# A streaming encoder layer on one core: stores issued by ScalarE, value matmuls of two heads paired, one compare split in two, projections copied out of PSUM first

## The chip, the core and the metric

One Trainium2 chip, one of its NeuronCores. The metric is the device time of one execution in microseconds (us), lower is better; shown are the median and the extremes of several executions, and one further execution that the hardware profiler recorded. Engines: PE (TensorE), DVE (VectorE), ACT (ScalarE), POOL (GpSimd), SP (SyncE, here only an issuer of DMAs).

## What is computed

One layer of an encoder for a prompt of 1024 rows (8 tiles of 128) and a decode batch of 8 x 16 rows (tile 8), model width 1024:

```python
n1 = rmsnorm(h); q_a,k_a,v_a,fl,q_b,k_b,v_b,gate_a,gate_b = split(n1 @ w_in)
y_a = forgetting attention, 8 heads x 64: softmax(q k / 8 + sum of log f) v, causal; decode reads a cache of 2048
y_b = chunk-band attention, 8 heads x 64: own chunk of 64 and the 8 before; decode reads a cache of 512
h += (sigmoid(gate_a) * (y_a @ w_up_a) + sigmoid(gate_b) * (y_b @ w_up_b)) @ w_out
h += PEER(rmsnorm(h))        # 128^2 single-neuron experts, 8 heads, the best 16 each
h += sigmoid(rmsnorm(h) @ w_ple_gate) * (p @ w_ple_proj)
```

q and k are normalised by head (sum of 64 squares). Outputs are y and the new rows of k, v and log f.

## The kernel before

The tiles go in two groups: group 0 is the decode tile 8 and tiles 0 to 2, group 1 is tiles 3 to 7. Each group has the stages norm, attention, merge and route; after both come expand (routing weights of tiles 3 to 7 spread into the table G_d in HBM), dense (all 16384 experts for tiles 3 to 7) and the last embedding step. On the trace: attention 0 fills 0 to 510 us, merge 0 510 to 700, route 0 and the norms of group 1 700 to 890, attention 1 890 to 1392, merge 1 1392 to 1700, route 1 1700 to 2020, expand 2020 to 2265, dense 2265 to 3875. A scheduler with a simulated clock sets the order of every engine's instructions from the code, priorities and buffer counts; on the chip each engine then runs its list in that order and stops at an instruction whose semaphores have not come.

**Attention.** Heads are worked in pairs, eight units, in the order 4, 0, 1, 5, 2, 6, 3, 7 (0 to 3 are pairs of the forgetting branch A, 4 to 7 of the band branch B). For each unit and tile, `project` (lines 301 to 352) multiplies the normed rows with the unit's 384 columns into a PSUM bank z (24 matmuls, lines 209 to 211; two banks in turn), lets ACT square the four 64-column heads of z with a sum (line 312), forms the factor on DVE and POOL, lets DVE write z times the factor to kq (line 314) and scale k (line 316), and then ACT copies v into vU (line 318). PE transposes k and q; ACT copies k into kT (line 345) and q, scaled, into qp (line 348). Stores of k and v to the outputs (lines 328, 329) and, in group 0, of kT and v to scratch that group 1 reads back (lines 350, 351) are issued by SP: 20 k, 20 v and 24 + 24 scratch stores in attention 0, 36 + 36 in attention 1, and 9 of log f. A unit's attention is interleaved with the projections of the next unit.

`prompt` (lines 452 to 499) does a tile's two heads one after the other: logits N, row minimum, exponential and division (lines 447, 449), transposes pt of the probabilities (line 494), their copy to pT (line 80), then the value matmuls of line 497: 128 rows x 64 columns of v stationary, 128 probabilities moving, one for each 128 keys, into the half `po[64h : 64h+64]` of a bank. `decode` does tile 8: kcd tiles of 256 KB come for the scores (line 522), then vcd tiles of 256 KB (line 586) for the value matmuls of line 591, which write four 32-row parts of one bank in turn. Both come through one ring of KC = 15 buffers, on SP's queue, and each DMA of either queue takes one of eight semaphores in turn, so that it waits for the DMA eight places earlier in the program.

**Elsewhere.** `setup_masks` builds on POOL, with lines 141 of `keep`, the selectors sel_p (128 x 8 x 128) used as the stationary operand of line 469. The 1024 row gathers of line 813 (a POOL DMA, then DVE lines 816 or 818) run at low priority wherever the order has room from 890 on; 400 of them stand before expand and the others in dense. In `expand_phase` DVE compares 128 x 1024 numbers at line 917 and 920, eighty times each; POOL (line 924) or ACT (line 929) turns the first into ga for PE (line 933); stage goes to G_d by a store on SP (line 939). Line 974 stores 36 tiles ge_d on SP, of work that fills PE in route 1 and expand.

## Time and profile before

| | us |
|---|---|
| median of 3 executions | 4042.02 |
| lowest and highest | 4021.49, 4048.87 |
| profiled execution, device time | 4036.04 |
| its span (first to last instruction) | 4033.9 |
| PE busy / DVE / POOL / ACT in the span | 3674.5 / 2939.1 / 1865.5 / 1446.2 |

[...] Busy times add what instructions of an engine cover; they say nothing of which engine the others waited for.

### The profile page before, as it was taken

The page shows a single profiled execution, that of the slowest core. Times are in us where ns is not written, and L with a number is a line of the kernel's source. Part 1 is how long each engine was busy: PE and PEld are TensorE (multiplying, and loading weights), DVE is VectorE, ACT ScalarE, POOL GpSimd, SP SyncE. Part 2 cuts the span into 40 slices and gives each one's busy share as a digit, 9 for nine tenths or more (in the row PEclk, how much of TensorE's full clock was granted, in tenths as well). Part 3 has the DMA queues.
Part 4 walks back from the last instruction along what each step waited for, and adds up shares of the span by engine and source line. Part 5 has one row for each costly group of instructions (what it writes and reads, how often), then busy time and mean ns, then how long its engine had stood idle before and what let it go on. Part 6 is the DMA issues. An engine that isn't in the chain of part 4 may idle for free.

```text
span 4033.9 us, 57386 instructions
## 1 busy us (share of the span) xinstructions
PE 3674.5 (91%) x20520; PEld 3032.9 (75%) x20520; DVE 2939.1 (73%) x5531; ACT 1446.2 (36%) x3307; POOL 1865.5 (46%) x1440
## 2 busy tenths in 40 slices
PE   7998899868888798899898899999999999999989
PEld 6555567656676565699898888888888888888866
DVE  5122202899887776889998698888888888888862
ACT  5444422346555510223488422222222222222231
POOL 5111032127667655553276355555555555555510
PEclk9999999879999999899999999999999999999999
DMA  6777733328888888983345789988989898989942
GB/s 207 239 237 208 229 96 120 103 74 262 276 284 263 285 317 297 329 268 115 109 189 219 274 307 310 320 311 310 330 313 317 307 325 314 325 302 307 313 159 72
DMA packets 415118, 1002.50 MB, mean 249 GB/s; under 512 B 38816, under 2 KB 170352, under 8 KB 412400
## 3 DMA queue, kind: packets, MB, share of 16 engines
q0 software_dynamic: 147456, 536.94, 38.7%
q1 hardware_dynamic: 267376, 461.90, 34.4%
q8 instruction: 161, 2.64, 0.3%
q14 instruction: 125, 1.02, 0.1%
HBM read 917.19 MB, written 81.50 MB: 248 GB/s over the span
## 4 chain that ended last, share of the span: by engine, by line
PE 30%; DVE 19%; DMA 19%; issue 18%; POOL 12%; ACT 2%; SPq 0%; POOLq 0%; DVEq 0%; ACTq 0%
DMA v<-in_pv,gi 7%; POOL u L813 6%; DMA u<-in_pu,gi 6%; PE hd L964 5%; POOL v L813 3%; DVE gya L818 3%; DVE u L816 3%; PE pg L933 3%; PE Sd L547 2%; PE py L1015 2%; PE py L1017 2%; PE py L1016 2%; PE pu L638 1%; DMA vs<-in_pv 1%; PE z L209 1%
## 5 line engine op out<-in xcount | busy, mean ns | idle before, releaser
L813 POOL DMA_INDIRECT v<-in_pv,gi x512 | 680.3, 1329 | 582.8 <-DVE gya L818 451.2
L813 POOL DMA_INDIRECT u<-in_pu,gi x512 | 663.4, 1296 | 505.7 <-DVE u L816 374.8
L816 DVE SCALAR_TENSOR_TENSOR u<-u,gn 128x1024 f32<-128x1024 f32 x512 | 628.2, 1236 | 169.0 <-DMA u<-in_pu,gi 167.3
L818 DVE SCALAR_TENSOR_TENSOR gya<-v,hid,gya 128x1024 f32<-128x1024 f32 x512 | 661.3, 1292 | 120.0 <-DMA v<-in_pv,gi 115.5
L1015 PE MATMUL py<-vh,wh 128*128 128x512 f32 x1280 | 507.7, 398 | 44.2 <-ACT wh L946 23.6
L964 PE MATMUL hd<-aTh,uh 128*128 128x320 f32 x2048 | 485.1, 314 | 24.0 <-ACT gp L967 13.7
L1017 PE MATMUL py<-vh,wl 128*128 128x512 f32 x1280 | 498.3, 395 | 5.8 <-DVE wl L947 5.5
L1016 PE MATMUL py<-vl,wh 128*128 128x512 f32 x1280 | 502.8, 394 | 0.0
L964 PE MATMUL hd<-aTh,ul 128*128 128x320 f32 x2048 | 484.1, 314 | 5.5 <-DVE ul L947 4.2
L964 PE MATMUL hd<-aTl,uh 128*128 128x320 f32 x2048 | 484.1, 313 | 0.0
L964 PEld LDWEIGHTS hd<-aTh,uh 128*128 128x128 f32 x2048 | 351.9, 191 | 35.1 <-ACT gp L967 15.0
L964 PEld LDWEIGHTS hd<-aTh,ul 128*128 128x128 f32 x2048 | 349.6, 190 | 12.6 <-DVE ul L947 6.9
L964 PEld LDWEIGHTS hd<-aTl,uh 128*128 128x128 f32 x2048 | 351.3, 191 | 4.0
L1015 PEld LDWEIGHTS py<-vh,wh 128*128 128x128 f32 x1280 | 242.9, 190 | 102.3 <-ACT wh L946 29.7
L946 ACT CAST vh<-vs 128x1024 fp32r<-128x1024 f32 x128 | 134.0, 1052 | 483.3 <-DMA vs<-in_pv 241.9
L1017 PEld LDWEIGHTS py<-vh,wl 128*128 128x128 f32 x1280 | 243.2, 190 | 61.2 <-DVE wl L947 10.6
L1016 PEld LDWEIGHTS py<-vl,wh 128*128 128x128 f32 x1280 | 242.9, 190 | 46.9
L946 ACT CAST uh<-us 128x1024 fp32r<-128x1024 f32 x128 | 134.2, 1048 | 293.0 <-PE hd L964 285.3
L946 ACT CAST wh<-ge 128x640 fp32r<-128x640 f32 x128 | 91.9, 727 | 402.7 <-DVE ge L993 213.4
L1018 DVE TENSOR_TENSOR yacc<-yacc,py 128x1024 f32<-128x1024 f32 x160 | 192.5, 1215 | 15.0 <-PE py L1017 15.0
L497 PE MATMUL po<-pT,vU 128*64 128x128 f32 x1056 | 153.0, 290 | 34.6 <-ACT pT L80 34.0
L933 PE MATMUL pg<-obb,ga 128*128 128x128 f32 x1280 | 158.8, 279 | 26.5 <-POOL ga L924 19.5
(1051 smaller groups left out, 7361.0 us busy)
## 6 DMA issues: line engine op xcount, KB each, us to landing
us<-in_uT SPq DMA_DIRECT2D x128, 512.0 KB
vs<-in_pv SPq DMA_DIRECT2D x128, 512.0 KB
G_d<-stage SPq DMA_DIRECT2D x10, 4096.0 KB
gj<-G_d SPq DMA_DIRECT2D x64, 640.0 KB
kcd<-in_kA SPq DMA_DIRECT2D x128, 256.0 KB
vcd<-in_vA SPq DMA_DIRECT2D x128, 256.0 KB
ge_d<-gp SPq DMA_DIRECT2D x36, 320.0 KB
ge<-ge_d SPq DMA_DIRECT2D x36, 320.0 KB
```

What stands on the lines that cost most here:

```text
L497: nc.tensor.matmul(po[64 * h:64 * h + 64, 0:P], vU[:, k0 + j, 64 * h:64 * h + 64], pT[:, j, :], start=j == 0, stop=j == nk - 1)
L547: nc.tensor.matmul(ps[32 * b4:32 * b4 + 32, :], q3[:, 4 * s + b4, :], rhs, start=br == 1 and q < nch, stop=True)
L813: nc.gpsimd.indirect_dma_start(out=r, out_offset=None, in_=I["pu" if k < P else "pv"], in_offset=bass.IndirectOffsetOnAxis(ap=gi[:, kk:kk ...
L816: nc.vector.scalar_tensor_tensor(r, r, 1.0, n2, op0=OP.mult, op1=OP.mult, accum_out=hid[:, kk:kk + 1])
L818: nc.vector.scalar_tensor_tensor(ya, r, hid[:, kk:kk + 1], ya, op0=OP.mult, op1=OP.add)
L933: nc.tensor.matmul(pg[:, c * P:(c + 1) * P], ga[:, b0 + c, :], ob[:, b0 + c, :], start=True, stop=True)
L946: nc.scalar.copy(out_h, src)
L964: nc.tensor.matmul(ps[sp][:, 0:Nw], a[:, k, :], b[:, k, sp * Nw:(sp + 1) * Nw], start=k == 0 and q == 0, stop=k == 7 and q == 2)
L1015: nc.tensor.matmul(py[:, c], wh[:, ns], vh[:, c], start=a, stop=False)
L1016: nc.tensor.matmul(py[:, c], wh[:, ns], vl[:, c], start=False, stop=False)
L1017: nc.tensor.matmul(py[:, c], wl[:, ns], vh[:, c], start=False, stop=z)
L1018: nc.vector.tensor_tensor(yacc[n], yacc[n], py, op=OP.add)
```

## The change

- Stores move from SP's queue to ACT's: k, v, kT, v to scratch, log f, G_d and ge_d (215 DMAs). The k store is placed behind the copy of kT.
- `project`: ACT copies z's first 256 columns to kq and the last 128 to vU at once; the squares read kq in SBUF and write a small shared tile sq (two buffers); DVE multiplies kq in place.
- `prompt`: both heads' probabilities are made first, and then the value matmuls of the two heads alternate for each 128 keys.
- sel_p is 128 x 8 and broadcast where it is used; the setup selects are 4 of 128 x 8 instead of 8 of 128 x 512.
- Ring KC 15 to 18, Dn one buffer instead of two, qp in group 0 six instead of eight.
- The compare of line 917 becomes two of 128 x 512.

```diff
@@ -28 +28 @@
-KC = 15
+KC = 18
@@ -95 +95 @@
-    sel_p = const.tile([P, 8, P], F32R, name="sel_p")
+    sel_p = const.tile([P, 8], F32R, name="sel_p")
@@ -163,3 +163,2 @@
-        for q in range(2):
-            t1 = tmp(f"t1{q}").rearrange("p (h c) -> p h c", h=4)
-            t2 = tmp(f"t2{q}").rearrange("p (h c) -> p h c", h=4)
+        t1 = tmp("t1")[:, 0:8]
+        t2 = tmp("t2")[:, 0:8]
@@ -167,5 +166,4 @@
-            o3 = one.rearrange("p (h c) -> p h c", h=4)
-            for t, off in ((t1, 4 * q), (t2, 32 + 4 * q)):
-                keep(t, o3, [[-1, 4], [0, P]], 0.0, -off, 1)
-                keep(t, t, [[1, 4], [0, P]], 0.0, off, -1)
-            nc.vector.tensor_tensor(sel_p[:, 4 * q:4 * q + 4, :], t1, t2, op=OP.add)
+        for t, off in ((t1, 0), (t2, 32)):
+            keep(t, one[:, 0:8], [[-1, 8]], 0.0, -off, 1)
+            keep(t, t, [[1, 8]], 0.0, off, -1)
+        nc.vector.tensor_tensor(sel_p, t1, t2, op=OP.add)
@@ -292 +290 @@
-                Dn = at.tile([P, 2, 256], F32, tag="Dn", name=f"Dn{g}{u}")
+                Dn = at.tile([P, 2, 256], F32, tag="Dn", name=f"Dn{g}{u}", bufs=1)
@@ -310,0 +309,4 @@
+            vt = vU[:, slot[t], :]
+            nc.scalar.copy(kq, z[:, 0:256])
+            nc.scalar.copy(vt, z[:, 256:384])
+            sq = at.tile([P, 64], F32, tag="sq", name=f"sq{nm}", bufs=2)
@@ -312 +314 @@
-                nc.scalar.activation(kq[:, 64 * h:64 * h + 64], z[:, 64 * h:64 * h + 64], AF.Square, accum_out=ss[:, h:h + 1])
+                nc.scalar.activation(sq, kq[:, 64 * h:64 * h + 64], AF.Square, accum_out=ss[:, h:h + 1])
@@ -314,2 +316,2 @@
-            nc.vector.tensor_tensor(kq.rearrange("p (h c) -> p h c", h=4), z[:, 0:256].rearrange("p (h c) -> p h c", h=4),
-                                    r.unsqueeze(2).broadcast_to([P, 4, 64]), op=OP.mult)
+            k4 = kq.rearrange("p (h c) -> p h c", h=4)
+            nc.vector.tensor_tensor(k4, k4, r.unsqueeze(2).broadcast_to([P, 4, 64]), op=OP.mult)
@@ -317,2 +318,0 @@
-            vt = vU[:, slot[t], :]
-            nc.scalar.copy(vt, z[:, 256:384])
@@ -328,2 +328 @@
-                nc.sync.dma_start(ko[rows, cu * P:(cu + 1) * P], kq[:, 0:P])
-                nc.sync.dma_start(vo[rows, cu * P:(cu + 1) * P], vt)
+                nc.scalar.dma_start(vo[rows, cu * P:(cu + 1) * P], vt)
@@ -333 +332 @@
-            qp = at.tile([P, 2, P], F32, tag="qp", name=f"qp{nm}", bufs=2 * nts if g == 0 else nts + 1)
+            qp = at.tile([P, 2, P], F32, tag="qp", name=f"qp{nm}", bufs=nts + 2 if g == 0 else nts + 1)
@@ -337,0 +337 @@
+                nc.scalar.dma_start(ko[rows, cu * P:(cu + 1) * P], kq[:, 0:P])
@@ -345,0 +346,2 @@
+                if ko is not None:
+                    nc.scalar.dma_start(ko[rows, cu * P:(cu + 1) * P], kq[:, 0:P])
@@ -350,2 +352,2 @@
-                    nc.sync.dma_start(kT_d[u, :, t * P:(t + 1) * P], kT[:, t * P:(t + 1) * P])
-                    nc.sync.dma_start(v_d[u, :, t, :], vt)
+                    nc.scalar.dma_start(kT_d[u, :, t * P:(t + 1) * P], kT[:, t * P:(t + 1) * P])
+                    nc.scalar.dma_start(v_d[u, :, t, :], vt)
@@ -413 +415 @@
-            nc.sync.dma_start(O["lf"][:, t * P:(t + 1) * P], lT[0:8, i, :])
+            nc.scalar.dma_start(O["lf"][:, t * P:(t + 1) * P], lT[0:8, i, :])
@@ -457 +459 @@
-        po = bank(f"po{nm}")
+        pTs = []
@@ -469 +471 @@
-                    nc.tensor.matmul(N[:, c0:c1], sel_p[:, 2 * u + h, :], cP[:, c0:c1], start=False, stop=not last)
+                    nc.tensor.matmul(N[:, c0:c1], sel_p[:, 2 * u + h:2 * u + h + 1].broadcast_to([P, P]), cP[:, c0:c1], start=False, stop=not last)
@@ -496,3 +498,6 @@
-            for j in range(nk):
-                nc.tensor.matmul(po[64 * h:64 * h + 64, 0:P], vU[:, k0 + j, 64 * h:64 * h + 64], pT[:, j, :],
-                                 start=j == 0, stop=j == nk - 1)
+            pTs.append(pT)
+        po = bank(f"po{nm}")
+        for j in range(nk):
+            for h, pT in enumerate(pTs):
+                r = slice(64 * h, 64 * h + 64)
+                nc.tensor.matmul(po[r, 0:P], vU[:, k0 + j, r], pT[:, j, :], start=j == 0, stop=j == nk - 1)
@@ -917,3 +922,3 @@
-                nc.vector.tensor_tensor(oa, iota_i.unsqueeze(1).broadcast_to([P, 2, P, 4]),
-                                        rb[:, 0, cw].rearrange("p (b c) -> p b c", b=2).unsqueeze(2).broadcast_to([P, 2, P, 4]),
-                                        op=OP.is_equal)
+                for b in range(2):
+                    nc.vector.tensor_tensor(oa[:, b, :, :], iota_i,
+                                            rb[:, 0, c0 + 4 * b:c0 + 4 * b + 4].unsqueeze(1).broadcast_to([P, P, 4]), op=OP.is_equal)
@@ -939 +944 @@
-                    nc.sync.dma_start(G_d[2 * n + c0 // 64], stage)
+                    nc.scalar.dma_start(G_d[2 * n + c0 // 64], stage)
@@ -974 +979 @@
-                nc.sync.dma_start(ge_d[q], ge)
+                nc.scalar.dma_start(ge_d[q], ge)
```

The order before and after, at three places. A name's digits are the group, the unit and the tile (of a prompt also the head); the number behind the underscore tells buffers apart.

SP's list in attention 0, where the second half of a decode step of unit 0 begins (kcd are keys, vcd values of the cache, out_vA, v_d and kT_d are stores of unit 1). Before:

```order
L522 DMA kcd0132_1399<-in_kA 128x512 [waits DMAHW3_49,PE_49]
L522 DMA kcd0133_1401<-in_kA 128x512 [waits DMAHW4_49,PE_49]
L329 DMA out_vA<-vU01_1158 128x128 [waits DMAHW5_49,Activation_49]
L329 DMA out_vA<-vU01_1158 128x128 [waits DMAHW6_49,Activation_49]
L351 DMA v_d_87<-vU01_1158 128x128 [waits DMAHW7_49]
L586 DMA vcd0000_1564<-in_vA 128x512 [waits DMAHW0_49,PE_49]
L350 DMA kT_d_86<-kT01_1157 128x128 [waits DMAHW1_49,Activation_49]
L586 DMA vcd0010_1566<-in_vA 128x512 [waits DMAHW2_49,PE_49]
L586 DMA vcd0020_1568<-in_vA 128x512 [waits DMAHW3_49,PE_49]
L586 DMA vcd0030_1570<-in_vA 128x512 [waits DMAHW4_49,PE_49]
```

After, the same place:

```order
L537 DMA bsd50_2770<-in_biasS 32x528 [waits DMAHW1_49]
L527 DMA kcd0132_1412<-in_kA 128x512 [waits DMAHW2_49,PE_49]
L527 DMA kcd0133_1414<-in_kA 128x512 [waits DMAHW3_49,PE_49]
L591 DMA vcd0000_1579<-in_vA 128x512 [waits DMAHW4_49,PE_49]
L591 DMA vcd0010_1581<-in_vA 128x512 [waits DMAHW5_49,PE_49]
L591 DMA vcd0020_1583<-in_vA 128x512 [waits DMAHW6_49,PE_49]
L591 DMA vcd0030_1585<-in_vA 128x512 [waits DMAHW7_49,PE_49]
```

The stores are gone from between the loads; they stand in ACT's list.

PE's list in attention 1 at unit 0, tile 4, before. The value matmuls of head 0 (reading pT1040) end here, those of head 1 (pT1041) come after its transposes pt104 and some other work:

```order
L497 MATMUL po104_10062<-pT1040_10076,vU10_9390 64x128 [waits Activation_49]
L468 MATMUL N1060_10277<-kT10_9389,qp106_9731 128x512 [waits Activation_49]
L469 MATMUL N1060_10277<-cP_92,sel_p_80 128x512
L468 MATMUL N1060_10277<-kT10_9389,qp106_9731 128x384
L494 MATMUL pt10410_10105<-ident_63,p1041_10099 128x128 [waits PE_49,Activation_49]
L494 MATMUL pt10410_10105<-ident_63,p1041_10099 128x128 x3
L469 MATMUL N1060_10277<-cP_92,sel_p_80 128x384
L471 LDWEIGHTS ident_b_68
L471 MATMUL N1060_10277<-m_diag_72,ident_b_68 128x128
L211 MATMUL z117_10342<-wu11h6_9915,aTl1_6516 128x384
L494 MATMUL pt10414_10111<-ident_63,p1041_10099 128x128 [waits Activation_49]
L497 MATMUL po104_10062<-pT1041_10104,vU10_9390 64x128 x4
```

After: the ten stand in one run behind both heads' transposes, and the first six rows of it, with what stands ahead, are

```order
L208 MATMUL z153_10580<-wu15l6_10567,aTh1_6572 128x384
L209 MATMUL z153_10580<-wu15h6_10566,aTl1_6573 128x384
L503 MATMUL po104_10189<-pT1040_10156,vU10_9457 64x128 [waits Activation_49]
L503 MATMUL po104_10189<-pT1041_10179,vU10_9457 64x128
L503 MATMUL po104_10189<-pT1040_10156,vU10_9457 64x128
L503 MATMUL po104_10189<-pT1041_10179,vU10_9457 64x128
```

The two heads alternate, and only the first of the ten and the last wait.

ACT's list in attention 0 at unit 1, tile 0, before (the squares of z010, with a copy of another tile's output among them):

```order
L312 ACTIVATE kq010_1311,ssz010_1312<-z010_1286 128x64 [waits DMAHW0_49,PE_49]
L312 ACTIVATE kq010_1311,ssz010_1312<-z010_1286 128x64
L499 COPY yT0_253<-po041_920 128x128 [waits PE_49]
L80 COPY pTd40_954<-ptd404_961 128x128 [waits PE_49]
L312 ACTIVATE kq010_1311,ssz010_1312<-z010_1286 128x64 x2
```

After:

```order
L310 COPY kq010_1322<-z010_1297 128x256 [waits DMAHW2_49]
L80 COPY pT0410_936<-pt04100_937 128x256 [waits PE_49]
L449 ACTIVATE p0420_1062,sm0420_1063<-N0420_1057,mn0420_1059 128x384
L352 DMA kT_d_86<-kT00_679 128x128 [waits Activation_49]
L80 COPY pT0411_950<-pt04110_951 128x256 [waits PE_49]
L347 DMA out_kA<-kq002_1031 128x128 [waits DMAHW1_49,DVE_49]
L449 ACTIVATE p0421_1078,sm0421_1079<-N0421_1073,mn0421_1075 128x384
L314 ACTIVATE sq010_1326,ssz010_1323<-kq010_1322 128x64 [waits Activation_49]
```

The copy of z010 stands first, two stores stand among the work on other tiles, and each square has a semaphore of its own engine to wait for.

The gathers: in both orders 400 stand before expand. By the end of merge 1, 354 of them stand in the order before and 337 in the order after, so that route 1 holds 46 before and 63 after.

## Rows read from the trace of the kernel before

**Rows 1.** Busy time by stage, the program's windows (us; counts in brackets).

```profile
core 0: us, PE busy (x) PEld busy (x) DVE busy (x) ACT busy (x) POOL busy (x), PEclk, DMA share, GB/s
0.00:510.00 510.00, 438.68 (x3418) 293.46 (x3419) 146.38 (x392) 253.37 (x838) 120.39 (x155) 0.96 0.74 223
...
890.00:1392.00 502.00, 442.68 (x2522) 341.63 (x2520) 422.57 (x819) 299.75 (x848) 352.44 (x299) 0.96 0.83 270
...
1700.00:2020.00 320.00, 290.51 (x1815) 281.73 (x1814) 295.61 (x1257) 112.34 (x188) 126.83 (x76) 0.94 0.52 173
2020.00:2265.00 245.00, 218.46 (x1734) 213.03 (x1733) 206.92 (x161) 199.77 (x518) 157.37 (x87) 0.99 0.50 202
2265.00:3875.00 1610.00, 1550.35 (x8200) 1371.25 (x8198) 1376.04 (x1517) 374.73 (x532) 850.01 (x621) 0.99 0.90 312
```

**Rows 2.** Waits of PE, 0 to 510: us in total, times, longest.

```profile
PE pod L591 <- DMA vcd<-in_vA: 25.6, 22, 2.4
PE z L209 <- ACT vU L318: 13.0, 3, 9.2
...
PE po L497 <- ACT pT L80: 7.6, 7, 1.4
```

**Rows 3.** Waits of SP's DMA queue, 0 to 510.

```profile
SPq L328 <- DVE kq L316: 22.7, 10, 6.1
SPq L351 <- ACT vU L318: 16.5, 8, 4.3
SPq L586 <- PE Sd L547: 15.3, 24, 1.6
SPq L350 <- ACT kT L345: 12.6, 12, 2.7
```

**Rows 4.** One store's issue (line 328): duration ns min/median/max.

```profile
L328 SPq DMA_DIRECT2D out_kA<-kq x36: 332/344/1157, 63.7 to 1276.5; - x36
```

**Rows 5.** Waits of PE, 890 to 1392.

```profile
PE po L497 <- ACT pT L80: 25.7, 22, 2.5
PE pt L494 <- ACT pT L80: 15.5, 13, 2.7
PE z L209 <- ACT vU L318: 9.6, 6, 4.4
```

**Rows 6.** PE's time in the value matmuls of line 497, by window.

```profile
0.00:510.00 510.00, 33.22 (x192) 21.14 (x192) 0.96 0.74 223
890.00:1392.00 502.00, 118.36 (x859) 95.58 (x857) 0.96 0.83 270
```

**Rows 7.** The same of line 591, the decode's value matmuls.

```profile
0.00:510.00 510.00, 58.40 (x1408) 43.85 (x1408) 0.96 0.74 223
```

**Rows 8.** Groups by shape, ScalarE: busy us, mean ns of one | idle before, releaser.

```profile
L312 ACT ACTIVATE kq<-z 128x64 f32<-128x64 f32 x288 | 60.7, 222 | 32.1 <-PE z L211 19.8 <-DVE fl L308 6.6 <-issue 4.4
L312 ACT ACTIVATION_READ_ACCUMULATOR kq<-z 128x1 f32 x288 | 58.1, 206 | 0.4
...
L715 ACT COPY sc<-sc 128x256 f32<-128x256 f32 x72 | 26.9, 373 | 130.7 <-DVE topi L732 112.7 <-PE sc L713 10.9 <-PE hd L964 4.6
```

**Rows 9.** The same, 0 to 510: one shape read from SBUF and from PSUM.

```profile
L449 ACT ACTIVATE p<-p,sm 128x384 f32<-128x384 f32 x16 | 10.2, 635 | 0.9 <-DVE sm L448 0.9
...
L447 ACT ACTIVATE p<-N,mn 128x384 f32<-128x384 f32 x16 | 9.5, 593 | 0.7 <-DVE mn L485 0.7
```

**Rows 10.** Selects of line 141 on GpSimd in the setup, ns min/median/max.

```profile
L141 POOL TENSOR_SCALAR_AFFINE_SELECT t<-one x4: 635/661/705, 25.9 to 28.1; 128x512 f32<-128x512 f32 x4
```

**Rows 11.** Groups by shape, VectorE.

```profile
L917 DVE TENSOR_TENSOR oa<-iota_i,rb 128x1024 bf16<-128x1024 bf16 x80 | 93.1, 1188 | 23.9 <-POOL ga L924 19.7 <-ACT rb L902 4.1
...
L789 DVE TENSOR_TENSOR oh<-oh 128x512 bf16<-128x512 bf16 x36 | 19.0, 529 | 0.1
```

**Rows 12.** Tile oa: the same compare, duration ns min/median/max.

```profile
L917 DVE TENSOR_TENSOR oa<-iota_i,rb x80: 676/693/2861, 2017.5 to 2250.4; 128x1024 bf16<-128x1024 bf16 x80
```

**Rows 13.** A gather's second VectorE instruction (the page's groups).

```profile
L818 DVE SCALAR_TENSOR_TENSOR gya<-v,hid,gya 128x1024 f32<-128x1024 f32 x512 | 661.3, 1292 | 120.0 <-DMA v<-in_pv,gi 115.5
```

## The prediction

> **What bounds the kernel now.** I read the table by stage first [rows 1], then what PE waited for in the two attention stages, since these are what the change touches, and then the durations of the pieces that are added or dropped. The table shows dense as a PE stage (1550 of 1610 us busy); nothing in it is edited, so I leave its time alone. In attention 0 PE is busy 439 of 510 us, in attention 1 443 of 502; the next engine there is DVE with 423 in attention 1, and ACT has 253 and 300. So PE sets both stages, with about 71 and 59 us of gaps in them. The gaps have names. In attention 0 the largest is the value matmuls of the decode waiting for a vcd load, 25.6 us in 22 pieces; then z waiting for the v copy of an older tile, 13.0 in 3, one of them 9.2 [rows 2]. In attention 1 they are short stops of value matmuls and transposes for a copy by ACT, 25.7 and 15.5 us, and again z, 9.6 [rows 5]. Route 1 is DVE's stage: 296 of 320 us. Expand has PE at 218 of 245, but part of that is the filling work of line 974, put there because it has room.
>
> **The change, part by part.** All sums are against the profiled execution, 4036.0 us (span 4033.9 and 2.1 around it); the median of the runs shown, 4042.0, lies 6 us above it, and what can be told from no change is about 1%, 40 us.
>
> *Stores leave SP.* SP's list is in order, and in attention 0 the stores stand between the vcd and kcd loads and wait for kq, v and kT: 22.7, 16.5 and 12.6 us of blocking, against 15.3 us that loads wait for a ring buffer freed by the decode scores [rows 3]. After the change the loads follow one another, and three more ring buffers let SP run further ahead. The most to gain is the 25.6 us of PE's stalls, the least nothing, if transfers and not their issue are late. Blocking of 51.8 us is more than the stall it stands before, so I take somewhat over half: -14 us.
>
> The DMA share of this stage is 0.74 [rows 1], so the transfers are not saturated in the mean. [...]
>
> *The same stores on ACT.* One issue is 344 ns [rows 4]: 92 in attention 0 make 31.6 us of ACT, 77 in attention 1 26.5. Their waits come with them; a k store behind the copy of kT finds its kq long finished, but each store also waits for the DMA eight places earlier, now mostly a load on the other queue. I count no wait here and put it into the rival below.
>
> *Projection.* One copy of 128 x 256 is added per unit and tile; the nearest row of that shape is 373 ns [rows 8], so 32 x 0.373 = 11.9 us in attention 0 and 40 x 0.373 = 14.9 in attention 1. The squares then read SBUF instead of PSUM. The same shape, 128 x 384, took 635 ns from SBUF and 593 from PSUM [rows 9], 42 ns apart: 128 squares make 5.4 us and 160 make 6.7. They also share a tile now, and each waits for the one before; between nothing and one accumulator read of 206 ns [rows 8] each, that is 0 to 59 us of ACT over both stages, of which I take nothing, as the order puts other instructions between them. ACT so gets 31.6 + 11.9 + 5.4 = 49 us in attention 0 and 26.5 + 14.9 + 6.7 = 48 in attention 1, where it has 257 and 202 us free. What hides it is that freedom. PE's waits for ACT are 13.0 + 7.6 = 21 us of 510 and 25.7 + 15.5 + 9.6 = 51 of 502 [rows 2, 5], 4 and 10% of the time in which ACT ends last; as the waits lengthen too I take 15% of the added time: +7 in each stage.
>
> [...]
>
> In exchange the v copy no longer stands behind the DVE's kq. The 9.2 us stop of z, in the first unit, should shrink most: with its neighbours I take -8 in attention 0. At later units the copy into vU waits for a unit's buffer anyway, so of the 9.6 us of attention 1 I take -3.
>
> *Paired value matmuls.* A record of line 497 takes PE 33.22 / 192 = 173 ns in attention 0 and 118.36 / 859 = 138 in attention 1 [rows 6]. Only half of the array's columns work. Decode's matmuls, which alternate over four parts of a bank, take 58.40 / 1408 = 41 ns each [rows 7]. For two alternating halves I take half of the present time, saving 17 and 59 us; the bounds are nothing (they run one behind the other) and the decode's 41 ns, which would save 25 and 83. Not all of it arrives: the pair now stands behind both heads' softmax, so that a tile's end waits for the second head's copy by ACT, and in the last tiles of a unit nothing else fills PE. I keep half: -9 and -29.
>
> *Setup.* Eight selects of about 0.65 us [rows 10], 5.2 us, become four small ones, on the way to the first decode scores: -3. The memory changes (Dn, qp) cost nothing as long as the qp of six suffices for four tiles and the next unit's; I take 0.
>
> *Gathers.* If attention 1 is shorter, the low-priority gathers find less room. The order has 63 instead of 46 in route 1: 17 more, at 1.29 us on DVE [rows 13] 22 us, where DVE is busy 296 of 320. I count half, +10; the bounds are 0 and 22.
>
> *Expand.* One compare becomes two. A 128 x 512 compare in bf16 took 529 ns in route [rows 11], so two make 1058. Before, the mean was 1188 [rows 11] but the median 693 [rows 12], with slow ones up to 2861: the change lies between (1058 - 1188) x 80 = -10 and (1058 - 693) x 80 = +29 us of DVE. The middle is +9; as PE's filling covers more than half of the stage I take +2. The stores of stage and gp no longer stop SP, which has loads for the filling behind them: 0 (to -3).
>
> *The sum.* Attention 0: -14 - 9 - 8 - 3 + 7 = -27. Attention 1: -29 - 3 + 7 = -25. Route 1 +10, expand +2. Together -40: 3996 us, and 4002 on the scale of the median. I forecast 3996.
>
> **The rivals.** *Everything arrives.* Pairing pays in full (-17 - 59), the vcd stalls go altogether (-25.6), the added ACT work is hidden, no gather is late: 4036 - 76 - 26 - 8 - 3 - 3 + 2 = 3922. For it: PE is the bound by 90%, and ACT is free almost half the time. Against: PE's waits in attention 1 are on ACT already. Chance 0.18.
>
> *ACT's queue stops at its stores.* The place is ACT's list in both attentions: 169 stores, each behind a load eight DMAs earlier which itself may wait for a ring buffer. Such a load waited 15.3 / 24 = 0.64 us [rows 3]; as much per store is 108 us in which no softmax step runs. If three quarters come out on PE, the time is 4036 - 40 + 81 = 4077. It decides once more than 37% of those waits (40 of 108) reach PE. For it: the pairing makes PE wait for ACT's last copy more than now. Against: a load issued eight places earlier has mostly landed. Chance 0.22.
>
> *Loads no sooner, and the time given back.* The vcd stalls stay, since transfers were late and not their issue (+14), and route 1 takes back all of attention 1's 25 instead of 10 (+15): 3996 + 29 = 4025, no change that can be measured. For it: the gathers are a fixed amount of DVE work. Against: DVE still has 79 us free in attention 1. Chance 0.10.
>
> **How the numbers follow.** The forecast's own case has 0.50, from about 3965 to 4030 by its bounds. Faster by over 1% means under about 4002: 0.30 of the forecast's 0.50 and all of the first rival make 0.48. Slower by over 1%, above 4082, is the upper part of the second rival and some of the unknown waits of the squares, 0.17. Within 1% remains 0.35. The range leaves out a tenth at either end: the lower end lies just above the first rival, 3925, the upper at the second, 4078.
>
> **What would show it.** Right: PE's waits for vcd fall below 12 us; line 503's records (the value matmuls after) take 70 to 90 ns; attention 0 ends near 483 and attention 1 is near 477 us long; ACT's busy time rises by about 39 us, and its queue's stores don't wait much. Wrong: records of the pair near 138 ns; ACT's queue rows with long waits at the stores and PE waiting for pT more than twice as long; route 1 longer by 20 us or more; expand longer than 255 us with DVE ahead of all. A gain in dense, which isn't edited, would mean that another mechanism is at work.

## The result, and the profile after

The changed kernel took 3991.45 us, median of 4 runs (3983.7 to 3994.9), against 4039.07 for the kernel before in the same comparison; the ratio is 0.9889, 95% interval 0.9869 to 0.9908. The profiled execution took 3992.5 us, 43.6 less than that of before; 3996 was forecast. The total came out close to the forecast; the experiments show that two of its largest terms were put in the wrong place, so that the closeness is in part luck.

The page's head and busy line of the changed kernel: PE lost 63 us of busy time, ACT gained 31.

```profile
span 3990.7 us, 57379 instructions
...
PE 3611.7 (91%) x20520; PEld 2990.8 (75%) x20520; DVE 2952.4 (74%) x5610; ACT 1477.4 (37%) x3379; POOL 1862.6 (47%) x1436
```

To see where the time went I took moments that exist in every version, each the first or last start of a tile's instructions. The tile view of the changed kernel (duration ns min/median/max, first and last start in us), in program order: decode outputs (the end of attention 0), scores of the routing (first in route 0, last in route 1), outputs of the prompt (the end of attention 1), the matmuls with w_up in the merges (the recorded expectations call them the matmuls of the gates), the compares and matmuls of expand, the sums of dense.

```profile
L599 ACT ACTIVATE obd<-pod,smd x16: 348/367/396, 96.5 to 466.3; 128x128 f32<-128x128 f32 x16
...
L718 PE MATMUL sc<-skbd,qT x144: 377/379/796, 711.1 to 1821.2; 128*128 128x256 f32 x144
...
L504 ACT COPY yT<-po x64: 241/265/295, 76.9 to 1325.6; 128x128 f32<-128x128 f32 x64
...
L643 PE MATMUL pu<-up,yT x288: 590/592/593, 473.0 to 1525.1; 128*128 128x512 f32 x144
...
L923 DVE TENSOR_TENSOR oa<-iota_i,rb x160: 409/419/2615, 1964.3 to 2199.0; 128x512 bf16<-128x512 bf16 x160
...
L938 PE MATMUL pg<-obb,ga x1280: 270/275/377, 1971.8 to 2206.1; 128*128 128x128 f32 x183
...
L1023 DVE TENSOR_TENSOR yacc<-yacc,py x160: 1206/1215/1222, 2261.4 to 3829.8; 128x1024 f32<-128x1024 f32 x160
```

Differences of such moments, here and from the same view of the kernel before:

| stretch | before, us | after, us | difference | forecast |
|---|---|---|---|---|
| start to the last decode output (attention 0) | 503.4 | 466.3 | -37.1 | -27 |
| to the first scores of route 0 (merge 0) | 244.9 | 244.8 | 0 | 0 |
| to the last prompt output (route 0, attention 1) | 643.6 | 614.5 | -29.1 | -25 |
| to the last w_up matmul (in merge 1) | 205.7 | 199.5 | -6.2 | 0 |
| to the last scores of route 1 | 275.3 | 296.1 | +20.8 | +10 |
| to the first compare of expand | 144.6 | 143.1 | -1.5 | 0 |
| expand | 239.0 | 241.8 | +2.8 | +2 |
| dense | 1617.9 | 1623.7 | +5.8 | 0 |

From there to the end of the span it is 159.5 and 160.9. The stages that answer to [rows 1], of the changed kernel:

```profile
core 0: us, PE busy (x) PEld busy (x) DVE busy (x) ACT busy (x) POOL busy (x), PEclk, DMA share, GB/s
0.00:473.00 473.00, 412.18 (x3418) 285.80 (x3419) 150.03 (x391) 268.90 (x870) 118.14 (x151) 0.96 0.80 240
840.00:1326.00 486.00, 402.94 (x2532) 305.23 (x2531) 417.34 (x884) 317.67 (x891) 333.00 (x287) 0.93 0.81 263
1627.00:1967.00 340.00, 307.67 (x1923) 297.70 (x1924) 327.14 (x1294) 116.91 (x195) 165.91 (x98) 0.95 0.59 196
```

Attention 0 moves its bytes at 240 GB/s where it was 223. Attention 1 has 403 us of PE in 486 where it had 443 in 502: PE has more gaps than before, though the stage is shorter. DVE's idle time tells more. Its largest waits in attention 1, before and then after, are for the rows that gathers load:

```profile
DVE gya L818 <- DMA v<-in_pv,gi: 30.8, 34, 1.8
DVE u L816 <- DMA u<-in_pu,gi: 30.8, 36, 2.1
...
DVE u L821 <- DMA u<-in_pu,gi: 32.6, 36, 2.9
DVE gya L823 <- DMA v<-in_pv,gi: 19.2, 24, 1.9
```

DVE is busy or stopped at a gather's load for 423 + 62 = 484 us of 502 before and 417 + 52 = 469 of 486 after. In route 1 it is busy for 327 of 340. PE's waits in attention 0, for [rows 2], then in attention 1, for [rows 5]:

```profile
PE po L503 <- ACT pT L80: 18.2, 9, 5.3
...
PE pod L596 <- DMA vcd<-in_vA: 3.5, 5, 1.2
...
PE z L207 <- ACT vU L311: 3.0, 2, 2.2
...
PE po L503 <- ACT pT L80: 15.2, 12, 4.4
PE pt L496 <- ACT pT L80: 14.4, 12, 3.1
```

The waits for vcd are gone but for 3.5 us, and those of the prompt's value matmuls for ACT's copy of pT have grown from 7.6 to 18.2. ACT's own waits in attention 0 hold a row that was not there before:

```profile
ACT pT L80 <- DMA vcd<-in_vA: 12.0, 4, 4.4
```

A copy of pT does not read vcd. What stood on ACT's queue ahead of it is a store, whose semaphore is that of a load eight places earlier; so I read the row as a store that stopped ACT, 12.0 us in four pieces. All rows of this kind together (an ACT instruction behind a load of the cache or of the decode's bias that it does not read) are about 32 us in attention 0, where before had 0.5; attention 1 has none.

The value matmuls of the prompt, for [rows 6]:

```profile
0.00:473.00 473.00, 27.93 (x192) 16.22 (x192) 0.96 0.80 240
840.00:1326.00 486.00, 66.84 (x864) 54.43 (x864) 0.93 0.81 263
```

That is 66.84 / 864 = 77 ns a record in attention 1 (138 before) and 145 in attention 0 (173). A record here is one matmul in the profile (its form there is 128*64, half the columns of the 128*128 of the scores above), and the figure is the time that PE is covered by them, divided by their number. One by itself lasts 273 ns in the median in both kernels and in e2 below; what changes is how far they overlap, and their ends are modelled by the profiler. ACT's groups by shape in the new projection, for [rows 8]:

```profile
L314 ACT ACTIVATE sq<-kq 128x64 f32<-128x64 f32 x288 | 73.8, 257 | 16.8 <-DMA kcd<-in_kA 3.8 <-DMA bsd<-in_biasS 2.2 <-ACT sq L314 1.7
...
L310 ACT COPY kq<-z 128x256 f32<-128x256 f32 x72 | 26.6, 370 | 20.7 <-PE z L209 10.8 <-DVE fl L306 5.9 <-DMA kcd<-in_kA 2.3
...
L314 ACT ACTIVATION_READ_ACCUMULATOR sq<-kq 128x1 f32 x288 | 55.3, 192 | 0.1
```

The copy costs 370 ns (373 was taken), a square from SBUF 257 instead of 222, 35 ns more where 42 were taken.

### The profile page after: what moved, and what is told of

It reads as the page before. It is cut to its first block, busy times and chain, and to the rows that moved or that the text cites. A ratio compares the mean times of both kernels' runs of the same rounds, so it can differ in the third digit from the quotient of the medians.

```text
span 3990.7 us, 57379 instructions
## 1 busy us (share of the span) xinstructions
PE 3611.7 (91%) x20520; PEld 2990.8 (75%) x20520; DVE 2952.4 (74%) x5610; ACT 1477.4 (37%) x3379; POOL 1862.6 (47%) x1436
## 4 chain that ended last, share of the span: by engine, by line
PE 25%; DVE 22%; issue 20%; DMA 19%; POOL 12%; ACT 1%; POOLq 0%; SPq 0%; ACTq 0%; DVEq 0%
DMA v<-in_pv,gi 9%; POOL u L818 6%; DMA u<-in_pu,gi 5%; POOL v L818 4%; DVE u L821 4%; DVE gya L823 3%; PE hd L969 2%; PE pg L938 2%; PE Sd L552 2%; POOL ga L929 2%; PE pu L643 1%; DMA vs<-in_pv 1%; PE z L207 1%; PE z L208 1%; PE py L1020 1%
## 5 line engine op out<-in xcount | busy, mean ns | idle before, releaser
L818 POOL DMA_INDIRECT v<-in_pv,gi x512 | 669.6, 1308 | 595.5 <-DVE gya L823 466.9
L818 POOL DMA_INDIRECT u<-in_pu,gi x512 | 675.8, 1320 | 499.1 <-DVE u L821 361.0
L821 DVE SCALAR_TENSOR_TENSOR u<-u,gn 128x1024 f32<-128x1024 f32 x512 | 642.2, 1262 | 175.1 <-DMA u<-in_pu,gi 172.1
L938 PEld LDWEIGHTS pg<-obb,ga 128*128 128x128 f32 x1280 | 153.0, 191 | 45.6 <-POOL ga L929 20.0
(1053 smaller groups left out, 7260.4 us busy)
```

The lines of the kernel that those rows point to most:

```text
L818: nc.gpsimd.indirect_dma_start(out=r, out_offset=None, in_=I["pu" if k < P else "pv"], in_offset=bass.IndirectOffsetOnAxis(ap=gi[:, kk:kk ...
L821: nc.vector.scalar_tensor_tensor(r, r, 1.0, n2, op0=OP.mult, op1=OP.mult, accum_out=hid[:, kk:kk + 1])
L938: nc.tensor.matmul(pg[:, c * P:(c + 1) * P], ga[:, b0 + c, :], ob[:, b0 + c, :], start=True, stop=True)
```

## The experiments

All were compared with the kernel before, which had a median of 4034 us in each of the three comparisons. The three stretches from the first scores of route 0 to the last of route 1 are added up in one column, for reasons that come below. Times by stretch are of one profiled execution each, the median of all runs; that execution can lie off the median (e7's took 3982 us, 15 below it, e1's and e4's 12 to either side).

| | median | ratio, interval | attention 0 | route 0 and attention 1 | merge 1 | route 1 | sum of the three |
|---|---|---|---|---|---|---|---|
| before | 4034 to 4039 | 1 | 503.4 | 643.6 | 205.7 | 275.3 | 1124.6 |
| after | 3991.5 | 0.9889 (0.9869 to 0.9908) | 466.3 | 614.5 | 199.5 | 296.1 | 1110.1 |
| e1, stores on SP | 3988.9 | 0.9902 (0.9871 to 0.9933) | 471.1 | 610.2 | 197.2 | 303.3 | 1110.7 |
| e2, unpaired | 3989.4 | 0.9906 (0.9870 to 0.9943) | 471.2 | 612.3 | 195.8 | 299.2 | 1107.3 |
| e3, old projection | 3998.7 | 0.9914 (0.9882 to 0.9946) | 470.7 | 613.6 | 201.1 | 293.8 | 1108.5 |
| e4, one compare | 3990.2 | 0.9900 (0.9867 to 0.9934) | 467.5 | 606.1 | 202.5 | 296.6 | 1105.2 |
| e5, before + new prompt | 4040.4 | 1.0012 (0.9993 to 1.0032) | 511.0 | 607.4 | 199.3 | 308.2 | 1114.9 |
| e6, after + old prompt | 4018.0 | 0.9966 (0.9943 to 0.9988) | 477.5 | 651.7 | 205.1 | 273.0 | 1129.8 |
| e7, before + memory edits | 3996.8 | 0.9911 (0.9881 to 0.9941) | 469.5 | 630.6 | 200.2 | 279.8 | 1110.6 |
| e8, 384 gathers | 3988.3 | 0.9891 (0.9856 to 0.9926) | 468.3 | 612.6 | 199.5 | 272.9 | 1085.0 |
| e9, ring of 15 | 4014.2 | 0.9957 (0.9937 to 0.9977) | 494.6 | 607.2 | 202.7 | 302.5 | 1112.4 |
| e10, e7 + new prompt | 3992.4 | 0.9911 (0.9876 to 0.9947) | 465.9 | 615.6 | 197.9 | 295.3 | 1108.8 |
| e11, e7 + stores on ACT | 3999.2 | 0.9920 (0.9900 to 0.9941) | 463.2 | 656.0 | 210.0 | 263.7 | 1129.7 |
| e12, 364 gathers | 3997.5 | 0.9921 (0.9897 to 0.9944) | 469.1 | 609.0 | 201.0 | 243.0 | 1053.0 |

The intervals are about 0.3% to either side, so medians under some 12 us apart are not told apart here.

**e1.** Every `nc.scalar.dma_start` of the changed kernel back to SP:

```diff
-                nc.scalar.dma_start(vo[rows, cu * P:(cu + 1) * P], vt)
+                nc.sync.dma_start(vo[rows, cu * P:(cu + 1) * P], vt)
...
```

> The changed kernel with every store back on SP, at the same places of the code. My theory: the stores between the loads made PE wait for vcd, so attention 0 (to the last decode output, 466 us in the changed kernel, 503 before) ends about 20 us later, near 486, PE's waits for vcd rise from 3.5 us to 15 or more, attention 1 stays within 5 us, and the time is about 4010. Rival (transfers were late, not their issue; ACT pays for its stores): attention 0 ends within 6 us of 466, attention 1 is 5 us or more shorter, the time is 3980 to 3992.

PE's waits in attention 0, largest first:

```profile
PE pod L596 <- DMA vcd<-in_vA: 16.6, 21, 2.5
...
PE po L503 <- ACT pT L80: 4.9, 7, 0.9
```

The waits for vcd came back, 16.6 us, as the theory had it, but those for pT went, 4.9 us instead of 18.2. Together they are 16.6 + 4.9 = 21.5 us with the stores on SP and 3.5 + 18.2 = 21.7 with the stores on ACT. Attention 0 ended only 4.8 us later and the median didn't move. Moving the stores turns waits for loads into waits for ACT, one for one. The theory's 20 us fall, and attention 0 and the median lie where the rival had them; its cost of ACT's stores in attention 1 is 4 us at most.

**e2.** The two loops around the value matmuls exchanged:

```diff
-        for j in range(nk):
-            for h, pT in enumerate(pTs):
+        for h, pT in enumerate(pTs):
+            for j in range(nk):
```

> The changed kernel with the value matmuls behind both heads' softmax as now, but all of head 0 and then all of head 1. My theory: alternation halves a record's time (77 ns now in attention 1, 138 before) and that is where attention 1's 29 us come from: records near 138 ns, attention 1 longer by 20 to 30 us, attention 0 by 3 to 8, and the time 4013 to 4025. Rival (attention 1 is shorter because both heads' softmax run before the value matmuls, or because z is copied early): attention 1 within 8 us, the time 3991 to 4000.

Line 503 by window, attention 0 and 1 (PE and PEld busy):

```profile
0.00:472.00 472.00, 34.09 (x192) 22.43 (x192) 0.96 0.78 238
845.00:1330.00 485.00, 92.02 (x844) 81.16 (x844) 0.96 0.81 263
```

The tile view, last prompt output:

```profile
L504 ACT COPY yT<-po x64: 242/266/298, 77.7 to 1332.1; 128x128 f32<-128x128 f32 x64
```

A record took 92.02 / 844 = 109 ns, 77 with alternation, and PE was 25 us busier in attention 1; the stretch was 2 us shorter, not 20 to 30 longer. My theory fell. Alternation does make the matmuls overlap more, but PE's time there does not decide. What is left of the new prompt is that both softmaxes stand ahead of the value matmuls, and the order of the gathers that comes with it.

**e3.** Squares and scaling on PSUM, v copied last, as before (the lines of `project` of the kernel before, with the stores on ACT).

> The changed kernel with the projection of before: squares and the scaling read z in PSUM, v copied last; stores stay on ACT. My theory: the early copy only helps the first unit, where z waited 9 us, and costs ACT 39 us that are mostly hidden: attention 0 longer by about 6 us, attention 1 by 0 to 3, the time 3991 to 4000. Rival (the early copy frees z and is a main part of the gain): attention 1 longer by 10 us or more, the time 4010 or more. Second rival (the added ACT work costs): attention 1 shorter by 5 us or more, the time 3980 or less.

Attention 0 was 4.4 us longer and attention 1 the same; 3999 cannot be told from 3991. The first rival, 10 us in attention 1, is out, and so is the second.

**e4.** The single compare of 128 x 1024 again.

> The changed kernel with the single compare of 128 x 1024. Expand took 239 us before from the first compare to the last matmul, 242 now. My theory: two compares cost VectorE a little more and expand is not bound by them all the way: expand 2 to 4 us shorter, the time 3987 to 3992. Rival (two compares let the first half of ga start earlier and save time): expand 3 us longer or more, the time 3995 or more.

Expand took 244.0 us, 2 longer instead of shorter, and the median is the same. The two ways are not told apart.

After these four none of the undone parts had cost what the forecast gave it, and the ring had not been touched. So the next four took parts alone, and the prompt as a whole.

**e5.** The kernel before with the new `prompt` (softmax of both heads, then alternating) and nothing else.

> The kernel before with the new prompt alone: both heads' softmax first, then alternating value matmuls. Its order holds 202 gathers by the end of attention 1 (220 before, 205 after). My theory now: attention 1 is shorter because this order leaves gathers out of it, and route 1 takes them back. From the first scores of route 0 to the last output of attention 1, 644 us before and 614 after, it takes 612 to 622; from the last matmul of the gates to the last scores of route 1, 275 before, it takes 290 or more; attention 0 ends between 495 and 503; the time is 4010 to 4030. Rival (the early copy or the stores are needed for it): the stretch of attention 1 stays above 635.

The tile view, last prompt output and last scores (643.6 and 275.3 before):

```profile
L502 ACT COPY yT<-po x64: 244/266/303, 85.3 to 1363.2; 128x128 f32<-128x128 f32 x64
...
L716 PE MATMUL sc<-skbd,qT x144: 377/379/795, 755.8 to 1870.7; 128*128 128x256 f32 x144
```

Attention 1's stretch is 36 us shorter, and route 1's is 33 longer; the time is that of before. This is the theory's picture with a larger gain (607.4 where 612 to 622 was expected) and a larger give-back; the end of attention 0, 511, and the time lie outside its ranges, and the 511 isn't explained. The new prompt by itself is worth nothing that can be measured.

**e6.** The changed kernel with the value matmuls behind each head's softmax again.

> The changed kernel with the prompt of before (value matmuls right behind each head's softmax). Its order holds 220 gathers by the end of attention 1, as before. My theory: the stretch of attention 1 goes back to 632 to 645 us, the end of route 1 is 15 to 20 us shorter, attention 0 ends within 6 us of 466, and the time is 3992 to 4005. Rival (the early copy and the stores on ACT shorten attention 1): the stretch stays within 8 us of 614.

```profile
L501 ACT COPY yT<-po x64: 244/266/293, 83.0 to 1375.6; 128x128 f32<-128x128 f32 x64
...
L715 PE MATMUL sc<-skbd,qT x144: 377/379/796, 723.9 to 1853.7; 128*128 128x256 f32 x144
```

The stretch went to 651.7 and route 1 to 273.0, both as in the kernel before, with its 220 gathers in the order. The length of attention 1 and route 1 is so explained, and the rival is out. But the sum of the three is 20 us above the changed kernel's, attention 0 is 11 longer, and 4018 is above the theory's range: with the stores and the projection on ACT, the old prompt costs 27 us.

**e7.** The memory edits alone:

```diff
-KC = 15
+KC = 18
-    sel_p = const.tile([P, 8, P], F32R, name="sel_p")
+    sel_p = const.tile([P, 8], F32R, name="sel_p")
-                Dn = at.tile([P, 2, 256], F32, tag="Dn", name=f"Dn{g}{u}")
+                Dn = at.tile([P, 2, 256], F32, tag="Dn", name=f"Dn{g}{u}", bufs=1)
...
```

> The kernel before with the ring of 18, the small sel_p and its setup, one Dn and six qp; stores, projection and prompt as before. My theory: the ring is the main part of attention 0's 37 us, since with stores back on SP the waits for vcd did not return: attention 0 ends at 472 to 485, PE's waits for vcd under 10 us (25.6 before), the time is 4005 to 4020. Rival (the stores or the early copy are enough by themselves, the ring adds nothing): attention 0 ends above 495, the time above 4028.

The premise of that text is wrong: the row of e1 shown above has the waits for vcd back. The test stands without it.

The last decode output in the tile view, and then PE's waits in attention 0:

```profile
L592 ACT ACTIVATE obd<-pod,smd x16: 367/368/380, 99.3 to 469.5; 128x128 f32<-128x128 f32 x16
```

```profile
PE pod L589 <- DMA vcd<-in_vA: 14.8, 14, 2.5
...
PE po L495 <- ACT pT L80: 8.7, 12, 1.4
```

Attention 0 ended at 469.5, 34 us earlier than before, by these edits alone, while PE still waited 14.8 us for vcd and 8.7 for pT. The time, 3997, is nearly all of the change. The end of attention 0 and the time lie below the theory's ranges, the waits for vcd above its 10 us. How much of it is the ring and how much the other memory edits this run does not tell; e9 takes the ring by itself.

**e9.** The counterpart: the changed kernel with KC = 15.

> The changed kernel with a ring of 15 buffers instead of 18, all else as changed. Before with the memory edits alone ended attention 0 at 469.5 us (503.4 before, 466.3 changed). My theory: it is the ring, which lets more of the cache's loads be under way: attention 0 ends at 485 or later and the time is 4005 to 4020. Rival (the setup, qp or Dn did it, or the stores off SP make up for a smaller ring): attention 0 ends by 475, the time within 6 us of 3991.

The waits of SP's queue in attention 0, first in the changed kernel:

```profile
SPq L591 <- PE pod L596: 29.2, 16, 8.3
...
SPq L527 <- PE Sd L552: 24.6, 20, 4.0
```

Then with the ring of 15, with PE's wait for vcd behind them:

```profile
SPq L527 <- PE Sd L552: 45.6, 39, 5.2
SPq L591 <- PE pod L596: 41.6, 19, 10.8
...
PE pod L596 <- DMA vcd<-in_vA: 20.3, 24, 2.4
```

The stage's row with the ring of 15 (columns as above):

```profile
0.00:495.00 495.00, 428.42 (x3403) 284.87 (x3403) 146.88 (x391) 268.20 (x867) 114.80 (x149) 0.96 0.75 227
```

Loads waited 45.6 + 41.6 us for a buffer that PE had still to read, 29.2 + 24.6 with 18 buffers; the stage moved 227 GB/s instead of 240, and attention 0 ended at 494.6, 28 us later. The median rose by 23 us. So with the stores on ACT the ring carries most of attention 0's 37 us, and 9 are left to the other edits together; with the stores on SP it was not tried alone (e1 and e7 both have 18 buffers). The median is still 20 us below before's, of which the table puts these 9 in attention 0 and 12 in the sum of the three.

**e10.** The kernel before with the memory edits and the new prompt.

> The kernel before with the memory edits and the new prompt, without the stores on ACT, the new projection and the two compares. My theory: this is all of the gain: attention 0 ends at 464 to 474, the stretch from the first scores of route 0 to the last of route 1 (1125 before, 1110 changed and with the memory edits alone) is 1104 to 1114, the time 3984 to 3998. Rival (the ACT edits bring 10 us or more): 4001 or more.

It has the changed kernel's times: 465.9, 1108.8 and a median of 3992. The stores on ACT, the early copy and the two compares bring nothing that can be measured on top of these two.

**e11.** e7 with its stores issued by ACT at the places of the code before.

> The kernel before with the memory edits and its stores issued by ACT, old prompt and old projection. The changed kernel with the old prompt was at 4018, before with the memory edits at 3997, so the stores and the projection together cost about 20 us where the old prompt is. My theory: half or more of it are the stores, since ACT stops at them while softmax steps wait: 4007 to 4018, the stretch from the first to the last scores 1118 or more. Rival (the projection's added copy and squares are the cost): 3990 to 4003.

PE's waits in attention 0:

```profile
PE po L495 <- ACT pT L80: 19.2, 10, 4.6
...
PE pod L589 <- DMA vcd<-in_vA: 3.8, 7, 1.2
```

The tile view, last prompt output and last scores:

```profile
L497 ACT COPY yT<-po x64: 246/266/307, 87.6 to 1363.9; 128x128 f32<-128x128 f32 x64
...
L711 PE MATMUL sc<-skbd,qT x144: 377/379/796, 707.9 to 1837.6; 128*128 128x256 f32 x144
```

The exchange of e1 shows again: with the stores on ACT PE waits 19.2 us for pT and 3.8 for vcd, 23.0 together; in e7 it was 8.7 and 14.8, 23.5 together. The sum of the three stretches is 1129.7, 19 us above e7's and the same as e6's, as the theory had it; the median, 3999, is in the rival's range and 2 us from e7's. Against e7 the medians say nothing, and the stretches are one execution each, e7's 15 us below its median. That stores on ACT cost attention 1 something under the old prompt is what the rows suggest; it is not settled. Nor is why the projection takes 14 us of attention 0 there (477.5 in e6, 463.2 here) and nothing under the new prompt.

**e8 and e12.** What route 1 gives back are gathers that attention 1's part of the order leaves out. Two versions of the changed kernel give them away to dense:

```diff
-G0 = 400
+G0 = 384
```

> The changed kernel with 384 gathers ahead of expand instead of 400, the other 640 in dense, which has a place for just 640. My theory: route 1 is paced by gathers on VectorE, and 16 fewer make it 16 to 21 us shorter; dense has room, at most 5 us longer: 3970 to 3980. Rival (dense pays for them one for one): 3986 to 3996.

```diff
-G0 = 400
-G1 = 5
+G0 = 364
+G1 = 6
```

> The changed kernel with 364 gathers ahead of expand and six instead of five in each of dense's 36 steps whose hidden layer was computed before, so that dense again ends its gathers three steps early. With 384 the stretch to the last scores was 25 us shorter, but the last stage 18 longer. My theory: the stretch is 30 us or more shorter than 1110, the last stage back at 156 to 158, dense at most 15 longer: 3955 to 3975. Rival (dense pays for each gather): dense 30 us longer or more, 3985 to 4000.

The tile view, first gather and last gather's sum (first and last start) in the changed kernel:

```profile
L818 POOL DMA_INDIRECT u<-in_pu,gi x512: 932/1275/3329, 860.3 to 3487.2; - x171
...
L823 DVE SCALAR_TENSOR_TENSOR gya<-v,hid,gya x512: 1254/1283/3380, 1154.8 to 3814.1; 128x1024 f32<-128x1024 f32 x171
```

The last gather's sum and the last sum of dense in e8:

```profile
L823 DVE SCALAR_TENSOR_TENSOR gya<-v,hid,gya x512: 1257/1281/1328, 1156.9 to 3820.8; 128x1024 f32<-128x1024 f32 x171
...
L1023 DVE TENSOR_TENSOR yacc<-yacc,py x160: 1203/1214/1223, 2233.3 to 3800.6; 128x1024 f32<-128x1024 f32 x160
```

The same in e12:

```profile
L823 DVE SCALAR_TENSOR_TENSOR gya<-v,hid,gya x512: 1256/1283/1352, 1158.3 to 3838.7; 128x1024 f32<-128x1024 f32 x171
...
L1023 DVE TENSOR_TENSOR yacc<-yacc,py x160: 1203/1214/1222, 2214.6 to 3782.2; 128x1024 f32<-128x1024 f32 x160
```

And PE's largest wait in e12's last stage:

```profile
PE zp L207 <- ACT aTgh L229: 49.4, 1, 49.4
```

Route 1 was 23 and 53 us shorter, dense was not longer (1620 and 1623), and yet the time is the same or a little worse: dense ends at 3801 and 3782 now, but the last gather comes at 3821 and 3839, later than the 3814 of the changed kernel, and PE waits 49 us for it. The times lie in the rivals' ranges, but not for their reason: it is not dense that pays but the last stage, which is 18 and 53 us longer. The theory of e12 had meant to bring that stage back and did not.

The price of a gather shows why. Counted by DVE's instructions in the traces, route 1 holds 81 gathers before, 99 in the changed kernel, 83 in e8 and 64 in e12, and takes 275, 296, 273 and 243 us: over all versions a straight line of 1.5 us a gather leaves less than 5 us unexplained. In dense, from the last matmul of expand to the last gather's sum, a gather takes 2.58 us in the changed kernel, 2.56 in e8 and 2.55 in e12, though e12's order has more of them to a step. So what is given away costs more where it goes: its stream outlasts dense. No version beat the changed kernel.

## Why the prediction was right, and where not

**The total, and the direction: right.** -40 was forecast, -43.6 measured in the profiled executions, with the parts of attention 0, attention 1 and route 1 each of the forecast's sign. None of the 37 us of attention 0 is given back; the stretches behind it add up to 6 us less. But attention 0 gained 10 us more than forecast and mostly by an edit that had no price, and route 1 gave back 11 more: that the sum is off by only 4 us is luck.

**"Stores leave SP" (-14): the wrong cause.** The rows of SP's blocking were read rightly and the waits for vcd did go when the stores left (3.5 us with them on ACT, 16.6 and 14.8 with them on SP). But they came back as waits for ACT (e1, e11), and e1 puts the stores' worth at 5 us of attention 0 and nothing in the time, near the prediction's lower bound; e9 puts the ring's at 28. The prediction named the three more buffers as an aside to the stores and gave them no price. The rows that spoke for them lay in the same view and were not among those I used. SP's largest waits in the kernel before, 0 to 510, are

```profile
SPq L522 <- PE Sd L547: 49.1, 45, 5.0
SPq L586 <- PE pod L591: 24.3, 23, 4.6
```

These are loads of kcd and vcd that wait for PE to free a buffer. The prediction set 15.3 us of such waits against 51.8 us of blocking by stores; with these two they are 89, more than the stores'. Such waits limit how many loads are under way: with 15 buffers the same two rows are 87.2 us in e9, with 18 they are 53.8. (The stage's rate, 223 to 240 GB/s, is no second proof: it is the same bytes in a shorter time.)

**"Paired value matmuls" (-9 and -29): the size of the edit right, its worth wrong.** 69 ns a record were taken in attention 1, 77 measured; in attention 0, 145 where 87 were taken. But e2 takes the alternation away, and attention 1 stays. What shortened the stage is the order that comes with the new prompt (e6: back to 652 without it), in which 15 fewer gathers stand up to the end of attention 1, by the lists of the versions. No run changes the gathers of this stage alone, but the traces speak for them. In the stretch of the table DVE carries out 224 gathers before and 209 after, 221 to 227 in all versions with the old prompt and 205 to 212 in all with the new one. Their instructions take 285 and 265 us of DVE and its waits for their loads 61 and 52, together 29 us less, which is what the stretch is shorter by. In every version DVE is busy or stopped at a gather's load for all but 10 to 27 us of it. So the step that failed is the first one, that PE sets the stage: of the 79 us in which DVE seemed free in attention 1, 62 were stops at gathers.

**"Gathers" (+10): too small.** 22 us was the bound and +20.8 came, with 18 more gathers in the stretch; for counting half the prediction gave no reason. In e5 the give-back was 33 of 36 us. The pattern shows in the sum of the three stretches: it is 1105 to 1115 or 1125 to 1130 in all versions with 400 gathers ahead of expand, though attention 1 varies by 50 us, and it falls only where gathers are taken out (1085, 1053). From the first gather's issue to the last one's sum it is 2954 us in the changed kernel, 2969 before, and 2937 to 2975 in all versions. So from 850 us to expand this kernel is a stream of gathers on DVE that everything else must fit beside, and time won in one of its stages is mostly paid back in the next. In dense the length alone proves less, since the order hands five gathers to each of its steps and PE is busy there as well. This is the third rival's mechanism, which had 0.10.

**Projection and ACT's added work (-8, -3, +7, +7): right in the sum.** z's wait for the v copy fell from 13.0 to 3.0 us in attention 0, of which e3 shows 4 us at the stage's end, and nothing in attention 1. The rival in which ACT stops at its stores has its mechanism in the trace, about 32 us of ACT's waits and the 18.2 of PE's, but not its price: 108 us of such waits were taken for both stages, and what there is only makes up for what the stores cost on SP. Where the old prompt stays (e6, e11) there may be more of it.

**Expand (+2): right in size**, +2.8, and e4 doesn't tell it from nothing. The two compares take 2 x 419 ns in the median, not the 1058 that were taken; the 529 ns of [rows 11] are no compare's, line 789 adds.

**Of the signs named ahead:** the waits for vcd, the record's time in attention 1 and expand came as for a right forecast. Attention 0 was shorter than named, and attention 1 longer (486 us by its windows, 477 named); ACT's busy time rose by 31 us, not 39. Two signs against it came too: route 1 was longer by 20.8 us, and in attention 0 PE waited for pT more than twice as long, 18.2 us after 7.6.

What stays open: why before with the new prompt has its attention 0 at 511, why dense, edited by nothing, takes 1604 to 1631 us in one execution or another, what the ring is worth with the stores on SP, and what sets the gathers' pace of about 2.55 us within dense.

## What to carry to other kernels

Where loads wait for a buffer that the consumer frees, count the ring before the queue (28 us of attention 0 here, the stores 5): with another issuer the consumer's wait for the load may only become a wait for that issuer (21.5 us of PE's waits for both with the stores on SP, 21.7 with them on ACT). Before an engine's idle time is counted as room, look up what it waits for: 62 us of DVE's 79 were part of the gathers. Where a fixed stream of low-priority work runs through several stages, price an edit over the whole length of that stream: a stage that gets shorter may only hand its share on (33 of 36 us in e5). A part of a change is shown to matter by undoing it from the new kernel and also by adding it to the old; here the memory edits alone gave nearly all of it (3997 against 3991), and only both directions showed that the ring was the larger part.

## What was unexpected of the hardware

A square of 64 columns on ACT with its sum took 257 + 192 ns from SBUF and 222 + 206 from PSUM: the longer source is partly made good by the read of the sum. And the value matmuls of attention 1, run in one piece but without alternation, covered 109 ns of PE each where between other work they covered 138; alternating between the two halves of the bank brought 77, though one by itself lasts 273 ns in the median each time.
